# Transformer block on one core: other places for the first operands of the second MLP product, the weight scales, one attention step and three squares

## The chip, the core and the metric

The kernel runs on one core of a Trainium2 chip. Its engines work side by side, each through its own queue of instructions: TensorE (PE in the profile) multiplies matrices, VectorE (DVE), ScalarE (ACT) and GpSimd (POOL) do the elementwise work, SyncE (SP) issues nearly all of the transfers. The metric is the device time of one execution in microseconds (us), the median of several runs.

## The reference

One block of a transformer over 1024 rows of width 1024, all in float32, then a last norm:

```
n = rms_norm(h, norm1_g)
qa, ka, va, qb, kb, vb = split(n @ w_in)
ya = mixer_a(qa, ka, va, sinks)      # sliding window, 8 heads on 2 kv heads
yb = mixer_b(qb, kb, vb, rel_bias)   # own chunk and 8 chunks before, 8 heads
y  = concat(rms_norm(ya, out_norm_a_g), rms_norm(yb, out_norm_b_g))
h  = h + y @ w_out
u  = square(relu(rms_norm(h, norm2_g) @ w_ff1))   # 1024 x 4096
h  = h + u @ w_ff2
return rms_norm(h, final_norm_g)
```

## The kernel before

Both MLP products are done in the manner of Strassen: seven products of half-size blocks in place of eight, numbered 1 to 7, with sums and differences of blocks as operands. Each operand is scaled by a power of two and split into a high and a low part in float16, and one product of such operands is 24 matmuls. The inner dimension of the MLP, 4096, is worked in eight groups n = 0 to 7 of 512. X names the operands from the rows of the normalised input (S, F their sums, `tp` the transposes that they come from); W and T those from the first weight; U those from u, the result of the first product; V and Z those from the second weight; C the sums of the output. `f` is the PSUM tile of the first product, `f_a` and `f_c` are those of the second.

The time falls into stages. Up to 376 us run the first projection and the two attentions, with the output projection of mixer A (`op_A`) interleaved with the last pair of heads of mixer B. Then come the projection of mixer B, the second norm, and the making of X, up to 463. From there to 729 runs the first MLP product, group after group, in the order 1, 5, 6, 3, 7, 2, 4 within a group (the groups 0 and 1 are interleaved). From 729 runs the second.

The two halves of group 7's products are followed by those of group 0 and 1 of the second product, whose operands must be there at 729: u for n = 0 and 1 (`u0_1` is u of group 0 as product 1 reads it), loaded back from the memory `ud`, where each group stored it, and blocks of the second weight (`w2_0_00` is block (0, 0) of group 0). `fetch2` issues a u load, `load2w` a weight load, and `prepare2(i)` the scaling and splitting of the i-th product's U and V: U's high part is made by ScalarE after it has scaled u (line 1416, 1418; under one line, 153, while in written order), U's low part by GpSimd (line 1420) or, for product 5, by VectorE, and V's low part by VectorE (line 1422). `m2` (in short m) are loads of the second weight from which only its largest entry is found, by squaring on ScalarE; they are issued by `look2`, one per product, and `scale2` makes the scale of them.

What sets the order: TensorE's instructions stand in the written order. Through the first product SyncE, and from its ninth product on ScalarE, are wrapped in `InOrder`, so that they issue as written too; VectorE, GpSimd and the rest go by a scheduler's estimate, with manual dependencies where the code adds one. A wait on such an engine holds all that stands behind it. In `product1`, VectorE adds product 6, 7 or 2 to the kept sum (line 1481) and squares what is above zero (line 1482).

Some further names: `ts_vB` is the second half of the values of the last pair of mixer B, times the row norm (line 443); `y` the output of mixer A, split for the projection (line 929 on VectorE, 926 on ScalarE); `o` its result (line 1077); `nm_B` the row maximum of the scores `S_B`; `G_B` the transposed probabilities and `VvB` the transposed values, both made by DMA. The function `scaled1` scales the weights of group n; `split` makes high and low part.

Of the kernel before, what the change touches and what calls it, by code (L numbers as in the profile page):

```python
# [35 lines left out]
AHEAD1 = 2  # L36
AT_ONCE = 3
AHEAD2 = 2
LOAD2 = 5
LOOK_AHEAD = 2  # L40
START_FILL = 3
A_FILL = 7
B_FILL = [13, 13, 9.5, 9.5] * 2 + [11.25] * 8
# [3 lines left out]
SPLIT_FIRST = {(1, 1, 2): 0, (1, 1, 5): 1}  # L47
SPLIT_AT = {(0, 0): (2, 0), (0, 2): (3, 0), (2, 1): (0, 1), (2, 3): (1, 1), (2, 5): (2, 1), (2, 7): (3, 1)}
POOL_NORM = ((1, 0), (1, 1))
FIRST_BLOCK = ((0, 0), (1, 0), (0, 1), (1, 1), (2, 0), (2, 1), (3, 0), (3, 1))  # L50
EARLY = 7
P_UP = 14
PLACES = ((4, 0, 6, 12), (0, 10, 20, 30))
# [6 lines left out]
def kernel(  # L60
# [37 lines left out]
    def f(ap):  # L98
        return ap.bitcast(F32)
# [324 lines left out]
                    for rep in range(2):  # L424
                        nc.sync.dma_start(f(dst[2 * hl + s][rep * HD : (rep + 1) * HD]), src)

    freed = []

    def behind_values(ins):

        if freed:
            dep = mybir.DependencyInfo(mybir.DependencyClass.NoSync, mybir.DependencyReason.DATA)
            tc.add_manual_dep(ins.ins, freed[0], dep, reason="program order")

    def values_b(acc, name, dst, t):

        if t == 0:
            if name == "vB3":
                halves[name] = page([P, 2, HALF], f"ts_{name}", F32)
            else:  # L440
                halves[name] = main.tile([P, 2, HALF], F32, tag="tst", bufs=TST, name=f"ts_{name}")
        st = halves[name]
        ins = nc.vector.tensor_tensor(st[:, t], acc, R1[:, t * HALF : (t + 1) * HALF], ALU.mult)
        if (name, t) == ("vB3", 1):
            freed.append(ins.ins.name)
        if t == 0:
            return
        st = st.rearrange("p a b -> p (a b)")
        top, e, up, down = (small.tile([P, 1], F32, tag=f"v{i}", bufs=2, name=f"{i}_{name}") for i in ("top", "e", "up", "down"))
        nc.vector.tensor_reduce(top, st, mybir.AxisListType.X, ALU.max, apply_absolute_value=True)  # L450
        nc.vector.tensor_scalar(top, top, 2.0**-90, None, ALU.max)
        nc.vector.tensor_scalar(e.bitcast(I32), top.bitcast(I32), 0xFF << 23, None, ALU.bitwise_and)
        nc.vector.tensor_scalar(
            up.bitcast(I32), e.bitcast(I32), -1.0, float((254 + V_UP) << 23), ALU.mult, ALU.add
        )
        nc.vector.tensor_scalar(
            down.bitcast(I32), e.bitcast(I32), 1.0, -float((V_UP + P_UP) << 23), ALU.mult, ALU.add
        )
        m = 4 + int(name[2:])
        gain = small.tile([P, 1], F32, tag="vgain", bufs=2, name=f"gain_{name}")  # L460
        nc.vector.tensor_tensor(gain, down, ogc[:, m : m + 1], ALU.mult)
        pieces = page([P, 2, SEQ], f"h{name}", F16)
        nc.scalar.activation(pieces[:, 0], st, AF.Copy, scale=up)
        nc.vector.scalar_tensor_tensor(pieces[:, 1], st, up, pieces[:, 0], ALU.mult, ALU.subtract)
        V = page([P, TB, 2, 2, HD], f"V{name}", F16)
        for s in range(2):
            for hl in range(2):
                nc.sync.dma_start_transpose(V[:, :, s, hl], pieces[s * HD : (s + 1) * HD, hl])
        dst.extend([V, down, gain])
# [349 lines left out]
    class UnitB:  # L819
# [96 lines left out]
        def end(self):  # L916
            p = self.pair
            y = p.rows(self.t)[self.s * HD : (self.s + 1) * HD]
            nc.scalar.activation(y, self.av[HD:], AF.Copy)
            behind_values(nc.vector.tensor_tensor(y, self.av[:HD], y, ALU.add))  # L920
            if self.s:
                p.finish(self.t)

# [38 lines left out]

    def split_ya(m, t):
        y = ys_a[m][t]
        behind_values(split_y(y, f(y[:, 1]), ogc[:, m : m + 1]))

    def out_weight(m):

# [81 lines left out]
    def out_proj_a():  # L1050
        ys, ws = ys_a, []
        for m in range(4):
            ys.append([load_ya(m, 0)])
        for m in range(4):
            ws.append(out_weight(m))
        yield
        for tb in range(TB):
            if tb == 1:
                for m in range(4):
                    ys[m].append(load_ya(m, 1))  # L1060
            h = hres[tb] = page([P, D], f"h{tb}", F32)
            nc.sync.dma_start(h, x[tb * P : (tb + 1) * P, :])
            ps = {}
            for n in range(8):
                q, dh = FIRST_BLOCK[n] if tb == 0 else (n % 4, n // 4)
                if (tb, n) in SPLIT_AT:
                    split_ya(*SPLIT_AT[tb, n])
                c = slice(dh * HALF, (dh + 1) * HALF)
                if q == 0:
                    ps[dh] = aps.tile([P, HALF], F32, tag="w", bufs=2, name=f"op_A_{tb}_{dh}")  # L1070
                out_proj_step(ps[dh], ys, ws, q, tb, c)
                last = (tb, n) == (TB - 1, 7)
                if last:
                    yield
                if q == 3:
                    o = main.tile([P, HALF], F32, tag="tst", bufs=TST, name=f"o{tb}_{dh}")
                    nc.scalar.activation(o, ps[dh], AF.Copy, scale=rA[:, tb : tb + 1])  # L1077
# [293 lines left out]
        nc.vector.tensor_tensor(down1[n], down1[n], xdown, ALU.mult)  # L1371
        to_scale1[n] = up1, [(0, 0), (0, 1), (1, 1), (1, 0)]

    to_scale1, last_w = {}, []

    def scaled1(n, *blocks):
        up1, left = to_scale1[n]
        for b in blocks:
            if b in left:
                left.remove(b)  # L1380
                w = w1s[(n, *b)]
                ins = act1[0].activation(w, w, AF.Copy, scale=up1)
                if last_w:
                    dep = mybir.DependencyInfo(mybir.DependencyClass.NoSync, mybir.DependencyReason.DATA)
                    tc.add_manual_dep(ins.ins, last_w[0], dep, reason="program order")

    def page1(shape, name, dt=F32):
        return page(shape, name, dt)
# [23 lines left out]
    def split(full, name, engine, alloc, up=None):  # L1412
        w = alloc(name)
        w = [w[:, hl] for hl in range(2)]
        if up is not None and engine is pool:
            act1[0].activation(full, full, AF.Copy, scale=up)  # L1416
            up = None
        last_w[:] = [act1[0].activation(w[0], full, AF.Copy, scale=1.0 if up is None else up).ins.name]  # L1418
        if up is None:
            engine.tensor_tensor(w[1], full, w[0], ALU.subtract)  # L1420
        else:
            engine.scalar_tensor_tensor(w[1], full, up, w[0], ALU.mult, ALU.subtract)  # L1422
        return w
# [19 lines left out]
    def product1(n, p):  # L1443
# [32 lines left out]
        if p == 4:  # L1476
            act1[0].activation(v, ps, AF.Relu)
            act1[0].activation(v, v, AF.Square)
            dve.tensor_reduce(top, ps, mybir.AxisListType.X, ALU.max)
        else:  # L1480
            dve.tensor_tensor_reduce(v, ps, v, 1.0, 0.0, ALU.add, ALU.max, top)  # L1481
            dve.scalar_tensor_tensor(v, v, 0.0, v, ALU.max, ALU.mult)
# [173 lines left out]
    for at, (n, p) in enumerate(order1):  # L1656
        if at == 8:
            act1[0] = InOrder(nc.scalar)
        if p == (1 if n > 1 else 5) and n:
            load1(n + 1)  # L1660
        ahead1 = at + (AHEAD1 + 1 if at < AT_ONCE else AHEAD1)

        behind = (n, p) == (0, 2)
        if ahead1 < len(order1) and not behind:
            prepare1(*order1[ahead1], ahead1)
        product1(n, p)
        for work in chores.get((n, p), ()):
            combined(*work)
            if behind and work[0] == 5:
                prepare1(*order1[ahead1], ahead1)  # L1670
        if 0 < n < NQ - 1:
            if p == 3:
                see1(n + 1)
            if p == 7:
                scale1(n + 1)
        if p == 3 and n and n % GQ == 0:
            scale_of_u(n // GQ - 1)
        if at > 6:
            look2(at, n < 2 or p not in (1, 5))
        if n == NQ - 1:  # L1680
            if p in (1, 5):
                for tile2 in blocks2(0)[(p == 5) * 4 :][:4]:
                    load2w(*tile2)
            if p == 6:
                for i in range(LOAD2 - 1):
                    fetch2(i)
            for i in {7: (0,), 2: (1, 2, 3)}.get(p, ()):
                prepare2(i)
    assert not to_see and not on_way and not to_scale
    act1[0] = nc.scalar  # L1690
    acc = {}
# [3 lines left out]
            acc[i, j, n] = page([P, 2, HALF], f"C{i}{j}{n}", F32)  # L1695
            queue[0].dma_start(acc[i, j, n], hB[2 * i + n][:, :, j * HALF : (j + 1) * HALF])

    for i in range(LOAD2 - 1, LOAD2):
        fetch2(i)
    load_acc(0, 0)  # L1700
    while stores:
        stores.pop(0)()
# [245 lines left out]
```

## Time and profile before

| | us |
|---|---|
| runs | 1044.37, 1043.99, 1040.94 |
| median of them | 1043.99 |
| profiled execution | 1042.79 |
| its span | 1041.0 |
| TensorE busy in the span | 1001.6 (96%) |
| VectorE busy | 810.6 (78%) |
| ScalarE busy | 645.0 (62%) |
| GpSimd busy | 446.8 (43%) |
| mean granted clock of TensorE | 0.989 |

A row of a timeline below reads: start and length in us, engine and line, operation, output <- inputs with their sizes, how many instructions are run together in the row, and in brackets the idle time before it and what ended that. SPq is SyncE's queue, whose rows are the issuing of transfers and not the transfers. A row of a group of issues ends with the size and the median time from issue to landing.

### The profile page before, as it was taken

The page shows a single profiled execution, that of the slowest core. Times are in us where ns is not written, and L with a number is a line of the kernel's source. Part 1 is how long each engine was busy: PE and PEld are TensorE (multiplying, and loading weights), DVE is VectorE, ACT ScalarE, POOL GpSimd, SP SyncE. Part 2 cuts the span into 40 slices and gives each one's busy share as a digit, 9 for nine tenths or more (in the row PEclk, how much of TensorE's full clock was granted, in tenths as well). Part 3 has the DMA queues.
Part 4 walks back from the last instruction along what each step waited for, and adds up shares of the span by engine and source line. Part 5 has one row for each costly group of instructions (what it writes and reads, how often), then busy time and mean ns, then how long its engine had stood idle before and what let it go on. Part 6 is the DMA issues. An engine that isn't in the chain of part 4 may idle for free.

```text
span 1041.0 us, 14050 instructions
## 1 busy us (share of the span) xinstructions
PE 1001.6 (96%) x4818; PEld 591.3 (57%) x4818; DVE 810.6 (78%) x1291; ACT 645.0 (62%) x1054; POOL 446.8 (43%) x341
## 2 busy tenths in 40 slices
PE   9999999999988999989999999999889999999997
PEld 7888887777655778534444444444334444444443
DVE  6576887867686748996999987984987877686976
ACT  8676766767585836663646654754487655657446
POOL 0466665243352562106435444543164343344333
PEclk9999999999998999999999999999899999999999
DMA  9944527999999985105767757748499544443004
GB/s 357 267 121 126 141 73 184 196 217 222 216 260 213 213 268 182 61 21 182 263 223 261 237 187 278 262 168 322 176 314 402 186 158 152 172 142 122 1 1 162
DMA packets 150567, 200.63 MB, mean 193 GB/s; under 512 B 78688, under 2 KB 96224, under 8 KB 150496
## 3 DMA queue, kind: packets, MB, share of 16 engines
q1 hardware_dynamic: 150352, 199.47, 63.0%
q8 instruction: 38, 0.62, 0.3%
q14 instruction: 33, 0.27, 0.1%
q10 hardware_dynamic: 144, 0.26, 0.1%
HBM read 120.01 MB, written 42.99 MB: 157 GB/s over the span
## 4 chain that ended last, share of the span: by engine, by line
PE 50%; DVE 7%; DMA 3%; ACT 3%; issue 2%; DVEq 0%; SPq 0%; ACTq 0%
PE f L173 24%; PE f_a L173 12%; PE f_c L173 6%; PE f_b L173 4%; PE op_B L173 2%; DMA u<-ud 2%; DVE V L1422 1%; DMA G_B<-H_B 1%; DMA w<-in_w_ff_dram 1%; DVE C L1741 1%; DVE Z L1392 1%; ACT V L1418 1%; DVE W L1422 0%; DVE h L1255 0%; ACT fo L1755 0%
## 5 line engine op out<-in xcount | busy, mean ns | idle before, releaser
L173 PE MATMUL f<-X,W 128*128 128x512 f16 x1344 | 294.3, 381 | 3.1 <-DVE X L1298 3.1
L173 PEld LDWEIGHTS <-U 128*128 128x128 f16 x1356 | 133.5, 99 | 171.8 <-issue 14.9
L173 PEld LDWEIGHTS <-W 128*128 128x128 f16 x1344 | 132.0, 98 | 160.3 <-issue 5.9
L1420 POOL TENSOR_TENSOR U<-u,U 128x1024 f16<-128x1024 f32 x48 | 117.7, 2462 | 176.7 <-ACT U L1418 152.8
L173 PE MATMUL f_a<-V,U 128*128 128x512 f16 x756 | 168.1, 383 | 4.8 <-DVE topf L1481 3.7
L1420 POOL TENSOR_TENSOR W<-T,W 128x1024 f16<-128x1024 f32 x29 | 73.6, 2541 | 87.1 <-ACT W L153 45.4
L1416 ACT ACTIVATE u<-u,uupn 128x1024 f32<-128x1024 f32 x46 | 52.0, 1143 | 65.8 <-DMA u<-ud 65.7
L173 PE MATMUL f_c<-V,U 128*128 128x512 f16 x384 | 86.0, 384 | 5.0 <-DVE C L1741 3.8
L1420 POOL TENSOR_TENSOR W<-w,W 128x1024 f16<-128x1024 f32 x21 | 49.5, 2359 | 87.6 <-ACT W L153 67.0
L1422 DVE SCALAR_TENSOR_TENSOR V<-Z,up,V 128x1024 f16<-128x1024 f32 x32 | 52.6, 1646 | 26.6 <-ACT V L1418 22.0
L635 ACT ACTIVATE P_B<-P_B,nm_B 128x640 f32<-128x640 f32 (+2 forms) x64 | 44.2, 690 | 30.8 <-DVE nm_B L632 16.4
L1418 ACT ACTIVATE U<-u 128x1024 f16<-128x1024 f32 x46 | 48.2, 1047 | 23.5 <-DVE Z L1392 11.3
L173 PE MATMUL op_A<-w_o,y 128*128 128x512 f32 x192 | 57.7, 427 | 4.9 <-ACT o L1077 3.8
L880 DVE SCALAR_TENSOR_TENSOR H_B<-P_B,rc_B,H_B 128x640 f16<-128x640 f32 (+2 forms) x64 | 51.8, 836 | 12.8 <-ACT H_B L875 12.5
L1422 DVE SCALAR_TENSOR_TENSOR V<-w,up,V 128x1024 f16<-128x1024 f32 x24 | 43.3, 1804 | 20.5 <-ACT V L1418 11.9
L153 ACT ACTIVATE w<-w,up 128x1024 f32<-128x1024 f32 x24 | 26.7, 1136 | 46.7 <-DVE up L1167 46.7
L173 PE MATMUL ip_qB<-nT,w_qB 128*128 128x512 f32 x192 | 53.8, 406 | 1.1 <-DVE t_kB L409 1.0
L173 PE MATMUL ip_kB<-nT,w_kB 128*128 128x512 f32 x192 | 53.7, 404 | 0.0
L173 PE MATMUL ip_vB<-nT,w_vB 128*128 128x512 f32 x192 | 51.2, 400 | 0.0
L173 PE MATMUL ip_qA<-nT,w_qA 128*128 128x512 f32 x192 | 50.2, 395 | 0.3 <-DVE VA L179 0.3
L173 PE MATMUL S_B<-KkB,QqB 128*128 128x320 f32 (+2 forms) x192 | 41.9, 328 | 7.3 <-DVE nm_B L634 4.7
L173 PE MATMUL op_B<-w_o,y 128*128 128x512 f32 x192 | 46.8, 396 | 0.2 <-ACT o L1077 0.2
(293 smaller groups left out, 1992.2 us busy)
## 6 DMA issues: line engine op xcount, KB each, us to landing
w<-in_w_ff_dram SPq DMA_DIRECT2D x64, 512.0 KB, 7.4
u<-ud SPq DMA_DIRECT2D x56, 512.0 KB, 6.0
ud<-k SPq DMA_DIRECT2D x48, 512.0 KB, 4.5
m<-in_w_ff_dram SPq DMA_DIRECT2D x32, 512.0 KB, 5.6
KkB<-t_kB SPq DMA_DIRECT2D x32, 256.0 KB, 5.3
xr<-in_x_dram SPq DMA_DIRECT2D x8, 512.0 KB, 8.6
st_o<-in_w_out_dram SPq DMA_DIRECT2D x8, 512.0 KB, 4.9
h<-in_x_dram SPq DMA_DIRECT2D x8, 512.0 KB, 4.8
```

What stands on the lines that cost most here:

```text
L153: ins = getattr(self.engine, op)(*args, **kw)
L173: pe(nc.tensor.matmul(*args, **kw))
L635: nc.scalar.activation(pr, pr, AF.Exp, bias=nm, scale=-1.0, accum_out=sm)
L880: nc.vector.scalar_tensor_tensor(lo, q, rc, hi, ALU.mult, ALU.subtract)
L1392: engine.tensor_tensor(t, a, b, op)
L1416: act1[0].activation(full, full, AF.Copy, scale=up)
L1418: last_w[:] = [act1[0].activation(w[0], full, AF.Copy, scale=1.0 if up is None else up).ins.name]
L1420: engine.tensor_tensor(w[1], full, w[0], ALU.subtract)
L1422: engine.scalar_tensor_tensor(w[1], full, up, w[0], ALU.mult, ALU.subtract)
L1741: nc.vector.scalar_tensor_tensor(flat(c), flat(ps), down2[g], flat(c), ALU.mult, ALU.add)
```

## The change

Four parts:

1. In group 7 of the first product, the first operands of the second are loaded in another order: u and the weight blocks interleaved, two of six u loads behind products 1 and 5 already, and all six ahead of group 7's stores (`FIRST_LOADS`; `LOAD2` is 6 instead of 5). The four first calls of `prepare2` follow products 6, 3, 7 and 2, not 7, 2, 2 and 2 (`FIRST_PIECES`).
2. `look2` loads m at six of seven products of every group, all but product 1, where it had been all seven in the groups 0 and 1 and five in the others.
3. Two orders are dropped that had been fixed by hand: `behind_values`, which held some y and Y work of VectorE behind `ts_vB`, and `FIRST_BLOCK`, the order of eight pieces of the output projection's first rows; and `last_w`, which held the scaling of a weight on ScalarE behind the last split.
4. The square in group 0 after products 3, 7 and 2 is a Relu and a Square on ScalarE instead of one operation on VectorE. In all, VectorE has three instructions fewer and ScalarE six more.

```diff
-LOAD2 = 5
+LOAD2 = 6
+FIRST_LOADS = {
+    1: ((0, ((0, 0, 0), (0, 0, 1))), (2, ())),
+    5: ((1, ((1, 0, 0), (1, 0, 1))), (3, ())),
+    6: ((None, ((0, 1, 1), (1, 1, 1))), (4, ())),
+    3: ((None, ((0, 1, 0), (1, 1, 0))), (5, ())),
+}
+FIRST_PIECES = {6: 0, 3: 1, 7: 2, 2: 3}
...
-FIRST_BLOCK = ((0, 0), (1, 0), (0, 1), (1, 1), (2, 0), (2, 1), (3, 0), (3, 1))
...
-            behind_values(nc.vector.tensor_tensor(y, self.av[:HD], y, ALU.add))
+            nc.vector.tensor_tensor(y, self.av[:HD], y, ALU.add)
...
-        behind_values(split_y(y, f(y[:, 1]), ogc[:, m : m + 1]))
+        split_y(y, f(y[:, 1]), ogc[:, m : m + 1])
...
-                q, dh = FIRST_BLOCK[n] if tb == 0 else (n % 4, n // 4)
+                q, dh = (n // 2, n % 2) if tb == 0 else (n % 4, n // 4)
...
-                ins = act1[0].activation(w, w, AF.Copy, scale=up1)
-                if last_w:
...
+                act1[0].activation(w, w, AF.Copy, scale=up1)
...
-            dve.scalar_tensor_tensor(v, v, 0.0, v, ALU.max, ALU.mult)
+            if n:
+                dve.scalar_tensor_tensor(v, v, 0.0, v, ALU.max, ALU.mult)
+            else:
+                act1[0].activation(v, v, AF.Relu)
+                act1[0].activation(v, v, AF.Square)
...
-            look2(at, n < 2 or p not in (1, 5))
+            look2(at, p != 1)
         if n == NQ - 1:
-            if p in (1, 5):
-                for tile2 in blocks2(0)[(p == 5) * 4 :][:4]:
+            for i, blocks in FIRST_LOADS.get(p, ()):
+                if i is not None:
+                    fetch2(i)
+                for tile2 in blocks:
                     load2w(*tile2)
-            if p == 6:
-                for i in range(LOAD2 - 1):
-                    fetch2(i)
-            for i in {7: (0,), 2: (1, 2, 3)}.get(p, ()):
-                prepare2(i)
+            if p in FIRST_PIECES:
+                prepare2(FIRST_PIECES[p])
...
-    for i in range(LOAD2 - 1, LOAD2):
-        fetch2(i)
```

**SyncE at the boundary.** The rows of SyncE's queue behind the last store of group 6 (`ud_3_152`), first before. The numbers behind the names count buffers; 108, 115, 112, 119 and 113, 120 are u of groups 0 and 1 for products 1, 5 and 6:

```order
L153 DMA ud_3_152<-k_6_6705 128x1024
L153 DMA w_0_00_6929<-in_w_ff_dram 128x2x512
L153 DMA w_0_01_6931<-in_w_ff_dram 128x2x512
L153 DMA w_0_11_6933<-in_w_ff_dram 128x2x512
L153 DMA w_0_10_6935<-in_w_ff_dram 128x2x512
L153 DMA w_1_00_6968<-in_w_ff_dram 128x2x512
L153 DMA w_1_01_6970<-in_w_ff_dram 128x2x512
L153 DMA w_1_11_6972<-in_w_ff_dram 128x2x512
L153 DMA w_1_10_6974<-in_w_ff_dram 128x2x512
L153 DMA u_1_7010<-ud_1_108 128x1024
L153 DMA u_1_7012<-ud_1_115 128x1024
L153 DMA u_5_7014<-ud_5_112 128x1024
```

After:

```order
L159 DMA ud_3_152<-k_6_6722 128x1024
L159 DMA u_1_6950<-ud_1_108 128x1024
L159 DMA w_0_00_6952<-in_w_ff_dram 128x2x512
L159 DMA w_0_01_6954<-in_w_ff_dram 128x2x512
L159 DMA u_5_6956<-ud_5_112 128x1024
L159 DMA u_1_6988<-ud_1_115 128x1024
L159 DMA w_1_00_6990<-in_w_ff_dram 128x2x512
L159 DMA w_1_01_6992<-in_w_ff_dram 128x2x512
L159 DMA u_5_6994<-ud_5_119 128x1024
L159 DMA w_0_11_7027<-in_w_ff_dram 128x2x512
L159 DMA w_1_11_7029<-in_w_ff_dram 128x2x512
L159 DMA u_6_7031<-ud_6_113 128x1024
```

The first u load was the ninth of these loads and is the first; the second u of product 1 was the tenth and is the fifth.

**ScalarE at the same place.** Before, from the last work of group 7's product 6; W_2 and W_4 are high parts for group 7's products 2 and 4:

```order
L153 ACTIVATE k_6_7005<-f_7_1_6897 128x1024
L153 ACTIVATE m_7_10_6889,tops_w_3_6629<-m_7_10_6889 128x1024
L153 ACTIVATE W_2_7018<-w_7_10_6588 128x1024
L153 ACTIVATE W_4_7050<-T_4_7048 128x1024
L153 ACTIVATE u_1_7010<-u_1_7010,uupn_5565 128x1024
L153 ACTIVATE U_1_7094<-u_1_7010 128x1024
L153 ACTIVATE V_1_7098<-w_0_00_6929,up_0_5758 128x1024
L153 ACTIVATE u_1_7012<-u_1_7012,uupn_5567 128x1024
L153 ACTIVATE U_1_7129<-u_1_7012 128x1024
L153 ACTIVATE V_1_7133<-w_1_00_6968,up_0_5758 128x1024
L153 ACTIVATE U_5_7138<-u_5_7014,uupn_5565 128x1024
```

After:

```order
L159 ACTIVATE k_6_7025<-f_7_1_6919 128x1024
L159 ACTIVATE u_1_6950<-u_1_6950,uupn_5570 128x1024
L159 ACTIVATE U_1_7033<-u_1_6950 128x1024
L159 ACTIVATE V_1_7037<-w_0_00_6952,up_0_5716 128x1024
L159 ACTIVATE W_2_7040<-w_7_10_6618 128x1024
L159 ACTIVATE u_1_6988<-u_1_6988,uupn_5572 128x1024
L159 ACTIVATE U_1_7076<-u_1_6988 128x1024
L159 ACTIVATE V_1_7080<-w_1_00_6990,up_0_5716 128x1024
L159 ACTIVATE W_4_7085<-T_4_7083 128x1024
L159 ACTIVATE U_5_7117<-u_5_6956,uupn_5570 128x1024
L159 ACTIVATE V_5_7120<-Z_5_7115,up_0_5716 128x1024
```

The high parts W_2 and W_4 stood ahead of the first u; each now stands behind the scaling, U and V of one half.

**ScalarE where X is made.** Before, from the scaling of group 1's first weights:

```order
L1382 ACTIVATE w_1_00_4527<-w_1_00_4527,up_1_4804 128x1024
L1382 ACTIVATE w_1_01_4529<-w_1_01_4529,up_1_4804 128x1024
L1418 ACTIVATE W_1_4811<-w_1_00_4527 128x1024
L1297 ACTIVATE X_4814<-S_0_4732 128x2x256
L1297 ACTIVATE X_4815<-S_1_4762 128x2x256
L1418 ACTIVATE W_5_4822<-T_5_4820,up_0_4587 128x1024
```

After:

```order
L1377 ACTIVATE w_1_00_4527<-w_1_00_4527,up_1_4804 128x1024
L1377 ACTIVATE w_1_01_4529<-w_1_01_4529,up_1_4804 128x1024
L1377 ACTIVATE w_1_11_4597<-w_1_11_4597,up_1_4804 128x1024
L1377 ACTIVATE w_1_10_4595<-w_1_10_4595,up_1_4804 128x1024
L1410 ACTIVATE W_1_4811<-w_1_00_4527 128x1024
L1292 ACTIVATE X_4814<-S_0_4732 128x2x256
L1292 ACTIVATE X_4815<-S_1_4762 128x2x256
L1410 ACTIVATE W_5_4822<-T_5_4820,up_0_4587 128x1024
```

The scalings of w_1_11 and w_1_10, which stood 29 and 33 rows further down, now stand ahead of W_1 and X.

**VectorE in the last attention pair.** Before:

```order
L632 ISA P_B_1_3_3538,nm_B_1_3453<-S_B_1_3_3537,b_B_587 128x640
L632 ISA nm_B_1_3453 128x1
L443 TENSOR_TENSOR ts_vB_3399<-ip_vB_1_3548,R_180 128x512
L929 SCALAR_TENSOR_TENSOR y_2_3405<-y_2_3405,ogc 128x512
L920 TENSOR_TENSOR Y_0_3472<-av_B_0_3494,Y_0_3472 64x512
L929 SCALAR_TENSOR_TENSOR y_3_3407<-y_3_3407,ogc 128x512
L450 TENSOR_REDUCE top_vB_3580<-ts_vB_3399 128x1
L634 ISA P_B_0_0_3612,nm_B_0_3607<-S_B_0_0_3611,b_B_586 128x128
```

After:

```order
L925 SCALAR_TENSOR_TENSOR y_2_3405<-y_2_3405,ogc 128x512
L876 SCALAR_TENSOR_TENSOR H_B_1_1_3490<-P_B_1_0_3458,rc_B_1_3455,H_B_1_1_3490 128x640
L876 SCALAR_TENSOR_TENSOR H_B_1_1_3490<-P_B_1_1_3482,rc_B_1_3455,H_B_1_1_3490 128x640
L628 ISA P_B_1_3_3538,nm_B_1_3453<-S_B_1_3_3537,b_B_587 128x640
L628 ISA nm_B_1_3453 128x1
L925 SCALAR_TENSOR_TENSOR y_3_3407<-y_3_3407,ogc 128x512
L916 TENSOR_TENSOR Y_0_3472<-av_B_0_3494,Y_0_3472 64x512
L441 TENSOR_TENSOR ts_vB_3399<-ip_vB_1_3548,R_180 128x512
L630 ISA P_B_0_0_3612,nm_B_0_3607<-S_B_0_0_3611,b_B_586 128x128
```

`ts_vB` moved behind y_2, y_3 and the addition to Y_0, and the pair's next scores (P_B_0_0) stand right behind it, ahead of the reduction of ts_vB.

More of the change, by code (lines that the diff above doesn't have):

```diff
@@ L425, in keys_b @@
                         nc.sync.dma_start(f(dst[2 * hl + s][rep * HD : (rep + 1) * HD]), src)
[L427 to L433, printed above, removed]
     def values_b(acc, name, dst, t):
@@ L442, in values_b @@
         st = halves[name]
-        ins = nc.vector.tensor_tensor(st[:, t], acc, R1[:, t * HALF : (t + 1) * HALF], ALU.mult)
-        if (name, t) == ("vB3", 1):
-            freed.append(ins.ins.name)
+        nc.vector.tensor_tensor(st[:, t], acc, R1[:, t * HALF : (t + 1) * HALF], ALU.mult)
         if t == 0:
@@ L1372, in scale1 @@
         to_scale1[n] = up1, [(0, 0), (0, 1), (1, 1), (1, 0)]
-    to_scale1, last_w = {}, []
+    to_scale1 = {}
     def scaled1(n, *blocks):
@@ L1381, in scaled1 @@
                 w = w1s[(n, *b)]
-                ins = act1[0].activation(w, w, AF.Copy, scale=up1)
-                if last_w:
-                    dep = mybir.DependencyInfo(mybir.DependencyClass.NoSync, mybir.DependencyReason.DATA)
-                    tc.add_manual_dep(ins.ins, last_w[0], dep, reason="program order")
+                act1[0].activation(w, w, AF.Copy, scale=up1)
     def page1(shape, name, dt=F32):
@@ L1417, in split @@
             up = None
-        last_w[:] = [act1[0].activation(w[0], full, AF.Copy, scale=1.0 if up is None else up).ins.name]
+        act1[0].activation(w[0], full, AF.Copy, scale=1.0 if up is None else up)
         if up is None:
```

## The prediction

> **What bounds the kernel now.** I read the page first, for the engines' shares.
>
> ```profile
> PE 1001.6 (96%) x4818; PEld 591.3 (57%) x4818; DVE 810.6 (78%) x1291; ACT 645.0 (62%) x1054; POOL 446.8 (43%) x341
> ```
>
> TensorE is the bound: an edit pays only where it removes idle time of PE, or a slow clock behind such idle time. So the second view is PE's timeline, which shows each run of matmuls, the idle time ahead of it and what ended that. Around the boundary of the two MLP products:
>
> ```profile
> 719.12 10.52 PE L173 MATMUL f<-X,W 128*128 128x512 f16 x48
> 729.48 2.75 PE L173 MATMUL f_a<-V,U 128*128 128x512 f16 x12
> 735.98 10.47 PE L173 MATMUL f_a<-V,U 128*128 128x512 f16 x36 [3.74 <-DVE topf L1481]
> 746.29 10.52 PE L173 MATMUL f_c<-V,U 128*128 128x512 f16 x48
> 767.89 2.75 PE L173 MATMUL f_c<-V,U 128*128 128x512 f16 x12 [0.47 <-DVE C L1741]
> 773.95 9.62 PE L173 MATMUL f_c<-V,U 128*128 128x512 f16 x36 [3.31 <-DVE C L1741]
> 783.40 8.80 PE L173 MATMUL f_a<-V,U 128*128 128x512 f16 x40
> ```
>
> A pair of products (48 matmuls) takes 729.48 − 719.12 = 10.36 us at full speed. Four pairs from 729.48 would end at 770.92, but the fifth starts at 783.40: 12.5 us are lost, 7.5 in the three waits shown and 5.0 at a slow clock. The third view, a table by stage (columns: length, PE, PEld, DVE, ACT and POOL busy, then the granted clock, DMA share and GB/s), shows the clock and the stage between:
>
> ```profile
> 463.00:719.00 256.00, 256.00 (x1193) 117.11 (x1192) 220.90 (x265) 145.79 (x177) 120.78 (x49) 1.00 0.66 228
> 310.00:320.00 10.00, 10.00 (x42) 6.75 (x42) 5.73 (x17) 7.63 (x18) 0.18 (x2) 0.83 0.97 191
> 330.00:340.00 10.00, 9.78 (x44) 7.26 (x45) 8.54 (x13) 7.52 (x15) 5.24 (x4) 0.83 1.00 227
> 440.00:450.00 10.00, 7.69 (x38) 3.52 (x36) 10.00 (x15) 5.46 (x7) 0.00 (x0) 1.00 0.00 2
> 450.00:460.00 10.00, 7.31 (x28) 2.87 (x25) 10.00 (x16) 6.09 (x10) 0.00 (x0) 0.83 0.13 52
> 730.00:740.00 10.00, 6.26 (x21) 2.37 (x20) 10.00 (x12) 6.30 (x7) 1.25 (x1) 0.72 0.00 1
> ```
>
> From 463 to 719 PE never stops; no edit there can gain. A granted 0.83 over 10 us costs 1.7 us, and it follows waits of over 2 us, as below.
>
> **The boundary, first loads ahead of the stores.** The 3.74 us are for a PSUM bank that the addition for product (7,2) frees on DVE. That stands behind V's low half, which waits for ScalarE, which waits for u:
>
> ```profile
> 706.71 5.26 SPq L153 DMA_DIRECT2D w<-in_w_ff_dram  x8
> 712.51 4.71 SPq L153 DMA_DIRECT2D u<-ud  x4
> w<-in_w_ff_dram SPq DMA_DIRECT2D x1, 512.0 KB, 5.7
> u<-ud SPq DMA_DIRECT2D x4, 512.0 KB, 10.7
> 723.63 1.15 ACT L153 ACTIVATE u<-u,uupn 128x1024 f32<-128x1024 f32 x1 [10.83 <-DMA u<-ud]
> 727.01 2.15 DVE L1422 SCALAR_TENSOR_TENSOR V<-w,up,V 128x1024 f16<-128x1024 f32 x1 [5.17 <-issue]
> 729.15 3.18 DVE L1392 TENSOR_TENSOR Z<-w,w 128x1024 f32<-128x1024 f32 x1
> 734.70 1.21 DVE L1481 CUSTOM_DVE_ANT_0 k<-f,k 128x1024 f32<-128x1024 f32 x1
> 725.95 2.13 POOL L1420 TENSOR_TENSOR U<-u,U 128x1024 f16<-128x1024 f32 x1 [9.81 <-ACT U L153]
> ```
>
> The rows with KB are DMA issues, with the median us to landing. The first 512 KB block issued at 706.71 lands at 712.4; the twelfth (the last u, issued about 717) at about 727.5, so one lands every 1.35 us. In the new order u0_1 is first and lands at 712.4 instead of 723.6, and u1_1 is fifth: 717.8. ScalarE then makes u (1.15), U (1.06) and V (1.13) for half 0 by 715.7, and the W of (7,2) by 716.8; for half 1 by 721.1, and the W of (7,4) by 722.1. DVE's part for (7,2) then runs at about 731 and not 734.70, one bank time after 729.48, so the 3.74 us shrink to 0–0.5. The next u's (product 6) are loaded ahead of the stores and no longer behind them, so the 0.47 and 3.31 us, which are C's additions late behind late U and V, go as well: by my walk C is done at 756–759, needed at 761.
>
> What it newly risks: the W of (7,2) and (7,4) stand on ScalarE behind the waits for u0_1 and u1_1, and their low halves on POOL behind U's (2.13 each). The low half of (7,2)'s W is ready at 716.8 + 2.13 = 718.9 or later, needed at 719.6; that of (7,4)'s at 724.2 or later, needed at 724.8. DVE and POOL delay one another here: the V row at 727.01 took 2.15 instead of 1.27 with a POOL row under way until 728.08. Three to four such DVE operations now fall between POOL's, 1.2 us each. I take 2.0 us of new waits on PE (bounds 0, the two free slots; 4, all four operations in series). Boundary: 12.5 − 0.5 − 2.0 = **10 us gained** (5.5 to 12).
>
> On SP the stores of group 7 stood behind twelve loads and now stand behind fourteen; only later products read them, and C's loads keep their place behind the first of them. LOAD2 = 6 brings one load of 512 KB forward, 1.35 us of the transfers: nothing.
>
> **m at six products.** The m blocks' loads, squares and scales come earlier; the amount of work is the same. Cover: the row 463:719, PE 256.00 of 256.00 with ScalarE busy 145.79. Cost 0. If a W came just in time, one more square and its read (1.05 + 0.19 by rows of their kind) would cost 1.24 us per group, 7.4 over six groups: the upper bound.
>
> **X stage: two scalings earlier, squares off DVE.**
>
> ```profile
> 442.76 0.63 PE L176 MATMUL tp<-ident,n 128*128 128x128 f32 x4 [1.89 <-DVE S L1325]
> 453.35 8.97 PE L173 MATMUL f<-X,W 128*128 128x512 f16 x33 [2.69 <-DVE X L1298]
> 431.34 2.19 ACT L1382 ACTIVATE w<-w,up 128x1024 f32<-128x1024 f32 x2 [0.60 <-DVE up L1167]
> 449.68 1.21 DVE L1482 SCALAR_TENSOR_TENSOR k<-k 128x1024 f32<-128x1024 f32 x1
> 451.42 1.28 DVE L1334 TENSOR_TENSOR S<-F,S 128x512 f32<-128x512 f32 x2
> ```
>
> DVE is busy 10.00 of 10.00 here, so PE's wait at 453.35 falls with whatever leaves DVE ahead of that X: the square (1.21) and two sums that now stand behind it (1.28), 2.5 us less. ScalarE gets 2.19 us of scaling ahead of W and X at 433, and a Relu and a Square (about 1.05 each) ahead of one X: I give back 0.5 on each path. PE then waits about 2.4 instead of 1.89 and 0.7 instead of 2.69, and with no long wait the clock of 450:460 stays at 1.00: 1.7. Sum: 2.0 − 0.5 + 1.7 = **3 us gained** (0.5, if ScalarE's work eats it, to 4). The two other squares (1.2 off DVE each, 2.1 on ScalarE) lie after 463, where nothing waits: 0.
>
> [...]
>
> **Attention: values' order put back.**
>
> ```profile
> 301.82 0.96 PE L173 MATMUL op_A<-w_o,y 128*128 128x512 f32 x3 [1.07 <-DVE ts_vB L443]
> 309.77 0.73 PE L173 MATMUL S_B<-KkB,QqB 128*128 128x512 f32 x2 [2.27 <-DVE nm_B L634]
> 330.22 0.96 PE L173 MATMUL op_A<-w_o,y 128*128 128x512 f32 x3 [3.81 <-ACT o L1077]
> 301.07 0.69 DVE L443 TENSOR_TENSOR ts_vB<-ip_vB,R 128x512 f32<-128x512 f32 x1
> 301.68 0.97 DVE L929 SCALAR_TENSOR_TENSOR y<-y,ogc 128x512 fp32r<-128x512 f32 x1
> 302.68 0.69 DVE L920 TENSOR_TENSOR Y<-av_B,Y 64x512 f32<-64x512 f32 x1
> 327.83 0.72 ACT L926 ACTIVATE y<-y,ogc 128x512 fp32r<-128x512 f32 x1 [3.78 <-DMA y<-ya]
> 329.50 0.67 ACT L1077 ACTIVATE o<-op_A,rgA 128x512 f32<-128x512 f32 x1
> 315.44 5.17 SPq L468 DMA_TRANSPOSE VvB<-hvB  x4
> ```
>
> The values' part (ts_vB) goes behind one y, then another, and Y: 301.07 becomes about 303, so the 1.07 us become about 3.7 and the slow clock comes at 300 instead of 310. The waits for nm_B behind it (2.27 and a smaller one of 1.0) shrink to about 0.5, since PE arrives 2.6 us later for the same DVE work. On SP the four VvB transposes (5.17) now stand ahead of a G_B transpose: 0–1.5 us. Up to 326 that is about even (+0.6). Then the 3.81 us: ScalarE's o stood behind a y that waited 3.78 for a DMA; now it stands ahead, so the wait and the 0.83 of 330:340 go: 3.8 + 1.7 − 0.6 = 4.9. As this stage has short slack on five queues, I take **3 us gained** (0 to 5).
>
> **Sum.** 10 + 3 + 3 = 16. The profiled execution took 1042.79 (span 1041.0 and 1.8 around it), so 1026.8; the median of the three runs shown is 1.2 above it, so **1028 us**.
>
> **Rivals.**
> 1. The boundary keeps half. If u0_1 lands 10.7 us after issue as the u rows above, and not 5.7, it comes at 717.4; the low W of (7,2) is ready at 724.5, needed at 719.6: a wait of 5 and 1.7 of clock. The boundary then gains 3.3, the sum is 9.3: 1034.7. For it: reading what was stored may be slower than a weight. Against: those u's had eight blocks ahead of them.
> 2. Attention does not gain: the wait for ts_vB comes with its slow clock (2.6 + 1.7), nm_B's waits stay, and G_B adds 1.5, while the 3.81 us turn into a wait for the y behind it. Instead of −3 it is +2: 1033.
> 3. Gains given back: 1 and 2 together, with no gain at X, is about −1.3: 1042.7, no change.
> 4. Slower: the W's behind u on ScalarE. If u0_1 is later by L than my 712.4, PE loses L and about 3.4 us of clock (both W's). That turns 16 us of gain into a loss at L = 13, with u0_1 at 725, 18 us after its issue. The nearest row is 10.7; it needs SP to be held up ahead of that load as well. At L = 18 it is 1049.
>
> **Chances.** As forecast 0.60 (1022 to 1033), rival 1 0.18, rival 2 0.10, rival 3 0.07, rival 4 0.05. The low end takes 12, 4 and 5 (21 less: 1023) and 1 for what the walk misses; the high end reaches rivals 1 and 2 with 2 us for m. About 0.3% (3 us) is what a measurement of this kernel can tell from no change. Faster by more: 0.60 + 0.18 + 0.10 = 0.88; within: 0.07; slower: 0.05.
>
> **What would show it.** Right: u0_1's scaling on ScalarE starts near 713, no wait over 1.5 us between 719 and 785 on PE, its clock there 1.00, the fifth pair 9–12 us sooner after the first; PE resumes at X after a wait below 1.5; no wait for o at 330. Wrong: PE waits for W inside (7,2) or (7,4); waits of 2 us or more for ts_vB and for nm_B; PE idle between 463 and 719.

## The result and the profile after

The changed kernel takes 1031.32 us (median of 4 runs, 1029.93 to 1032.67), the kernel before 1043.09 in the same comparison: a ratio of 0.990, with a 95% interval from 0.9879 to 0.9922. The medians differ by 11.8 us; the ratio stands for 10.4. 1028 was forecast, with 1022 to 1033 for the case as forecast and up to about 1037 with rivals 1 and 2. A profile is of one execution: the one of the changed kernel took 1032.67, the longest of its four, with a span of 1030.9, so the two spans differ by 10.1 us, and the parts below are made up against that. The page's row for the engines' shares:

```profile
PE 998.8 (97%) x4818; PEld 592.0 (57%) x4818; DVE 799.7 (78%) x1288; ACT 650.6 (63%) x1060; POOL 447.2 (43%) x341
```

TensorE is busy 2.8 us less with the same matmuls: that is mostly slow clock that went (mean granted clock 0.992, before 0.989). The rest is idle time. PE's timeline at the boundary, as read before:

```profile
699.78 22.83 PE L179 MATMUL f<-X,W 128*128 128x512 f16 x105
726.43 7.03 PE L179 MATMUL f<-X,W 128*128 128x512 f16 x24 [3.83 <-DVE topf L1473]
733.30 10.52 PE L179 MATMUL f_a<-V,U 128*128 128x512 f16 x48
764.38 10.52 PE L179 MATMUL f_c<-V,U 128*128 128x512 f16 x48
774.74 10.52 PE L179 MATMUL f_a<-V,U 128*128 128x512 f16 x48
```

Inside the second product all is as forecast: from 733.30 each pair follows the last after 10.36 us, without a wait, and at full clock. But one product earlier, ahead of (7,4), stands a wait that the forecast does not have: 3.83 us, for the addition (line 1473) that frees a PSUM bank, and 24 matmuls in 7.03 us and not 5.2 behind it. Product 4 adds to the PSUM tile that product 7 has written, so it cannot start before the addition for product 7 has read that tile. (Such additions are made on VectorE for the products 3, 7 and 2; product 6 is copied by ScalarE.) The other waits of PE of over 0.8 us between 300 and 600:

```profile
304.48 2.93 PE L179 MATMUL op_A<-w_o,y 128*128 128x512 f32 x6 [4.03 <-DVE ts_vB L441]
345.39 0.85 PE L179 MATMUL S_B<-KkB,QqB 128*128 128x320 f32 x4 [1.64 <-DVE nm_B L628]
369.22 0.48 PE L179 MATMUL av_B<-G_B,VvB 128*128 128x384 f16 x2 [1.22 <-DMA G_B<-H_B]
439.57 0.66 PE L182 MATMUL tp<-ident,n 128*128 128x128 f32 x4 [1.97 <-ACT F L1312]
507.28 20.46 PE L179 MATMUL f<-X,W 128*128 128x512 f16 x94 [0.87 <-POOL W L1412]
592.02 0.32 PE L182 MATMUL all_w<-ident,top_w 128*128 128x128 f32 x1 [1.68 <-DVE top_w L1189]
```

The wait for o at 330 and the one for X at 453 are gone; ts_vB waits longer; and at 507 and 592, in the stage where PE never stopped before, stand two new ones.

Why the bank was late is read from the three engines' timelines at that place, VectorE first, then GpSimd and ScalarE, and last the u load's row of DMA issues:

```profile
712.67 2.21 DVE L1414 SCALAR_TENSOR_TENSOR V<-w,up,V 128x1024 f16<-128x1024 f32 x1 [7.16 <-ACT V L159]
719.02 3.15 DVE L1384 TENSOR_TENSOR Z<-w,w 128x1024 f32<-128x1024 f32 x1
722.10 3.14 DVE L1414 SCALAR_TENSOR_TENSOR V<-w,up,V 128x1024 f16<-128x1024 f32 x1
725.16 1.21 DVE L1473 CUSTOM_DVE_ANT_0 k<-f,k 128x1024 f32<-128x1024 f32 x1
...
718.54 2.55 POOL L1412 TENSOR_TENSOR U<-u,U 128x1024 f16<-128x1024 f32 x1 [1.67 <-ACT U L159]
721.05 3.10 POOL L1412 TENSOR_TENSOR W<-T,W 128x1024 f16<-128x1024 f32 x1
...
709.30 1.15 ACT L159 ACTIVATE u<-u,uupn 128x1024 f32<-128x1024 f32 x1 [1.18 <-DMA u<-ud]
...
u<-ud SPq DMA_DIRECT2D x1, 512.0 KB, 4.5
```

The u load itself came sooner than forecast: it was issued at 704.82 and not 706.71, and landed 4.5 us later and not 5.7. The addition for product 7 of group 7 needs product 7, which ended at about 717.4, and a kept sum that was long there. It stood on VectorE behind Z and V of the second piece, which nobody needs before the second product, and each of these took over 3 us, beside an operation of GpSimd, where such operations take 1.2 elsewhere.

By stage, from the waits above and those of before (a half clock for 3.4 us, called a dip below, costs 1.7). The wait near 980 is this one of the kernel before:

```profile
981.64 10.52 PE L173 MATMUL f_c<-V,U 128*128 128x512 f16 x48 [1.24 <-ACT V L1418]
```

| stage | lost before | lost after | gained | forecast |
|---|---|---|---|---|
| attention, 299 to 400 | 8.5 + 3.4 of clock | 7.1 + 3.4 | 1.4 | 3 |
| X | 5.0 + 1.7 | 2.0 + 1.7 | 3.0 | 3 |
| first product, 463 to (7,2) | 0 | 2.55 | -2.55 | 0 |
| boundary | 12.5 | 3.8 + 1.7 | 7.0 | 10 |
| second product, near 980 | 1.2 | 0 | 1.2 | 0 |

The sum is 10.05, the spans differ by 10.1. Each row compares one execution with one other; how far that carries for attention is said further down.

### The profile page after: what moved, and what is told of

Same layout as the page of the kernel before. It is cut to its first block, busy times and chain, and to the rows that moved or that the text cites. A ratio compares the mean times of both kernels' runs of the same rounds, so it can differ in the third digit from the quotient of the medians.

```text
span 1030.9 us, 14057 instructions
## 1 busy us (share of the span) xinstructions
PE 998.8 (97%) x4818; PEld 592.0 (57%) x4818; DVE 799.7 (78%) x1288; ACT 650.6 (63%) x1060; POOL 447.2 (43%) x341
## 4 chain that ended last, share of the span: by engine, by line
PE 46%; DVE 7%; issue 4%; DMA 3%; ACT 2%; POOL 2%; SPq 0%; DVEq 0%; POOLq 0%; ACTq 0%
PE f L179 17%; PE f_a L179 14%; PE f_c L179 7%; PE f_b L179 4%; PE op_B L179 2%; DMA w<-in_w_ff_dram 2%; POOL W L1412 2%; DVE X L1293 1%; DMA G_B<-H_B 1%; DVE T L1384 1%; DVE W L1414 1%; DVE V L1414 1%; DVE Z L1384 1%; PE op_A L179 1%; DVE h L1250 0%
## 5 line engine op out<-in xcount | busy, mean ns | idle before, releaser
L1412 POOL TENSOR_TENSOR U<-u,U 128x1024 f16<-128x1024 f32 x48 | 119.9, 2509 | 166.8 <-ACT U L1410 152.7
L179 PE MATMUL f_a<-V,U 128*128 128x512 f16 x756 | 165.3, 379 | 1.0 <-DVE C L1734 1.0
L1410 ACT ACTIVATE V<-Z,up 128x1024 f16<-128x1024 f32 x30 | 34.1, 1138 | 20.7 <-DVE Z L1384 20.1
```

Of the source, the lines that this page charges most:

```text
L179: pe(nc.tensor.matmul(*args, **kw))
```

## The experiments

Each ratio is to the kernel before in the same comparison; the changed kernel's is 0.990, with 2.2 us to either side, so differences of 2 or 3 us from it are not clear of the intervals. All edits are to the changed kernel unless the text says otherwise.

**Part 1 undone** (the loads and pieces of before):

```diff
-            for i, blocks in FIRST_LOADS.get(p, ()):
...
+            if p in (1, 5):
+                for tile2 in blocks2(0)[(p == 5) * 4 :][:4]:
+                    load2w(*tile2)
+            if p == 6:
+                for i in range(LOAD2 - 1):
+                    fetch2(i)
```

> The changed kernel with its first part undone: the loads, the pieces and LOAD2 = 5 of before at the boundary; m at six products, attention and X as changed. Theory: the first part took 12.5 us of loss away and put a wait of 3.8 us and 1.7 us of slow clock in, so 7 us net, and another 1.2 us late in the second product: undone, about 1039 us, with the waits of 3.7 and 3.3 us back and no wait of 3.8 us ahead of product (7,4). Rival: the 3.8 us wait comes from m or from the phase of the stage and stays: 1043 us or more.

Measured 0.9959 (0.9945 to 0.9973), 1039.7 us. PE's timeline:

```profile
732.77 10.78 PE L179 MATMUL f_a<-V,U 128*128 128x512 f16 x36 [3.23 <-DVE topf L1473]
770.60 7.93 PE L179 MATMUL f_c<-V,U 128*128 128x512 f16 x36 [3.30 <-DVE C L1737]
979.61 10.70 PE L179 MATMUL f_c<-V,U 128*128 128x512 f16 x41 [3.08 <-DVE C L1737]
```

The two old waits are back and the new one ahead of (7,4) is gone, as the theory has it: the wait of 3.83 us belongs to part 1. With 0.006 of 1043 us, part 1 is worth about 6 us, less than the 7.0 and 1.2 of the table, and the wait at 979 is part of it. At 979 stands a wait of 3.08 us where the changed kernel has none.

**Part 2 alone**, on the kernel before:

```diff
-            look2(at, n < 2 or p not in (1, 5))
+            look2(at, p != 1)
```

> The kernel before with only the second part of the change: m at six of seven products. Theory: it costs the two new waits in the first product, 0.9 and 1.7 us, so 1045.5 us against 1043. Rival: those waits come from the three earlier parts, which shift PE against VectorE in that stage; then m alone has no wait between 463 and 719 and takes 1043 us, no change.

Measured 1.0012 (0.9997 to 1.0026): the time does not tell the theories apart, nor a loss from none; the timeline does in part.

```profile
596.35 0.32 PE L183 MATMUL all_w<-ident,top_w 128*128 128x128 f32 x1 [1.68 <-DVE top_w L1200]
```

The 1.68 us come with part 2 and nothing else: the transpose `all_w`, which PE runs for the scale that m gives, stands at 596.35 and waits, where in the kernel before the same transpose starts at 604.40 without a wait. The wait of 0.87 for W does not appear here, nor in the next two kernels, so it is not m's alone; with part 1 undone it is there, at 0.89. What else it needs stays open.

**Part 3's attention orders put in again** (`behind_values` and `FIRST_BLOCK`).

> The changed kernel with the two hand-made orders of the attention stage put in again (VectorE's y work behind the values, and the order of the first eight pieces). Theory: the two together gained 2 us, so 1033.3 us, with the waits of 1.1, 2.3 and 3.8 us back, and with 3.4 us of slow clock as before. Rival: the forecast 3 to 5 us: 1035 us. Second rival: the later stages absorb it and the time stays at 1031.

Measured 0.9921 (0.9892 to 0.9949), 2.2 us more than the changed kernel's ratio. That is the theory's size, but the intervals overlap and hold the two rivals too. The waits of 1.62 for ts_vB, 0.96 and 2.96 for nm_B and 3.25 for o are back; a wait of 2.89 at 979.06 is there as well, so not all of the 2.2 need be attention's.

**The X stage of before** (`last_w`, and the squares on VectorE).

> The changed kernel with the third scaling order and the squares on VectorE put in again (X stage as before). Theory: worth 3.0 us: 1034.3 us, with the wait for X of about 2.7 us back and the slow clock moved behind it. Rival: ScalarE's extra work eats it, and it is worth 0.5 us or less: 1031.5.

Measured 0.9954 (0.9939 to 0.9969): 5.6 us by the ratios, more than expected.

```profile
451.50 8.75 PE L179 MATMUL f<-X,W 128*128 128x512 f16 x32 [2.69 <-DVE X L1293]
978.25 12.04 PE L179 MATMUL f_c<-V,U 128*128 128x512 f16 x48 [3.09 <-DVE C L1733]
```

The wait for X is back with its clock, the 3.0 us of the theory. The rest is the second row: the wait near 979 again, with 1.7 us of clock. By the ratios the three parts undone come to 6.2, 2.2 and 5.6 us, 14.0 in all, and the whole change to 10.4 with m's loss of 1.2 to add: 2.4 too much, which the intervals do not clear of noise. The traces show what would count twice: three of these kernels wait about 3 us near 979, where the changed kernel doesn't wait. The orders of VectorE, ScalarE and GpSimd in the second product are the same in x3_old_attention as in the changed kernel, so it isn't an order; what sets that wait was not found.

**Is the wait the bank?** VectorE's work for the first pieces held behind the bank's addition, and the second piece prepared after product 7, so that (7,4)'s W stands ahead of u1_1 on ScalarE:

```diff
-FIRST_PIECES = {6: 0, 3: 1, 7: 2, 2: 3}
+FIRST_PIECES = {6: (0,), 7: (1,), 2: (2, 3)}
...
+            added = dve.tensor_tensor_reduce(v, ps, v, 1.0, 0.0, ALU.add, ALU.max, top)
+            if (n, p) == (NQ - 1, 7):
+                bank_free.append(added.ins.name)
...
+        if engine is dve and bank_free and len(bank_free) == 1:
+            dep = mybir.DependencyInfo(mybir.DependencyClass.NoSync, mybir.DependencyReason.DATA)
+            tc.add_manual_dep(ins.ins, bank_free[0], dep, reason="program order")
```

> The changed kernel with V, U and Z work of VectorE for the first second-product pieces held behind the addition of group 7's product 7, which frees the bank for product (7,4); the second piece is prepared one product later, so that W of (7,4) stands ahead of u1_1 on ScalarE. Theory (the 3.83 us wait is the bank, held by VectorE's queue): no wait of over 1 us ahead of product (7,4), clock 1.00, 5.5 us less than the changed kernel: ratio to before 0.985, 1025.5 to 1028 us on the first chip's scale. Rival: the boundary is bound by the landing of u and the sum of work on VectorE; then the wait reappears ahead of the second product (f_a or f_c, 3 us or more) and the time stays at 0.990.

Measured 0.9899 (0.9862 to 0.9936): no gain. The wait ahead of (7,4) is gone and the second product starts at 726.37, but then:

```profile
758.49 2.75 PE L179 MATMUL f_c<-V,U 128*128 128x512 f16 x12 [0.88 <-DVE C L1742]
771.98 12.17 PE L179 MATMUL f_a<-V,U 128*128 128x512 f16 x48 [2.58 <-DVE C L1742]
```

0.9, 0.2 and 2.6 us and 1.7 of clock are 5.4, where the changed kernel lost 5.5. The cause of the wait was right, what it is worth was wrong: the rival's half held, for a wait inside the second product and not ahead of it. VectorE is busy 42 of 45 us from 735 to 780 in both. This suggests that the second product of the changed kernel runs without a wait in part because the bank has made PE late for it. (The edit also holds back VectorE's work for the first pieces; r3_squares7, further down, does not, and waits for C as well.)

**GpSimd out of the way, first try.** The low half of U for the second piece issued later:

```diff
+        if name == "U1_1":
+            later.append(lambda: engine.tensor_tensor(w[1], full, w[0], ALU.subtract))
...
+        while later and p == 7:
+            later.pop()()
```

> The changed kernel with one operation of GpSimd moved: the low half of U for the second piece (half 1, product 1) is issued behind product 7's work, so GpSimd is idle while VectorE makes Z and V ahead of the bank's addition; VectorE's order is the same. Theory (VectorE's two-input operations wait while GpSimd runs one, 1.9 us each here): Z takes 1.2 instead of 3.15 us, the addition at 725.2 comes 3 us earlier, and the wait ahead of product (7,4) falls from 3.8 to about 1 us. Rival (VectorE is late for its inputs, ScalarE's V or the loads): Z's and V's ends stay, and the wait stays over 3 us.

Measured 0.9913 (0.9887 to 0.9938). GpSimd still ran that operation first (at 718.16, ahead of W's at 720.97), and the wait was 4.2 us. The edit did not do what it should, so it tells nothing of the cause.

**More work off VectorE.** The squares of group 7 on ScalarE too:

```diff
-            if n:
+            if 0 < n < NQ - 1:
                 dve.scalar_tensor_tensor(v, v, 0.0, v, ALU.max, ALU.mult)
```

> The changed kernel with the fourth part carried to group 7: its three squares are a Relu and a Square on ScalarE as well, and the scheduler then puts the addition that frees the bank for (7,4) ahead of V of the second piece. Theory (at the boundary VectorE's sum of work bounds, and moving a wait only passes it on): 3.6 us and more leave VectorE between 715 and 735, the boundary's loss falls from 5.5 to 1 to 2 us: ratio to before 0.986, against 0.990 for the changed kernel. Rival (the loads of u bound the boundary): the loss stays at 5 us or more, in other places: 0.990.

Measured 0.9943 (0.9922 to 0.9964), 4.5 us more than the changed kernel's ratio: the theory of VectorE's sum fell in this form. VectorE's work between 705 and 735 did fall, from 22.8 to 17.2 us, and the addition no longer holds the bank, but PE then waits inside the second product (2.15, 1.59 and 0.2 us for C). Then the six low halves of U on VectorE:

```diff
-            split(a, f"U{n}_{p}", dve if p == 5 else pool, high, uup[n]), split(b, f"V{n}_{p}", dve, high, up2[g])
+            split(a, f"U{n}_{p}", dve if p == 5 or 3 < at < 10 else pool, high, uup[n]), split(b, f"V{n}_{p}", dve, high, up2[g])
```

> As r3_squares7, with the low halves of U for products 6, 3 and 7 of the second product's first group (six operations) on VectorE instead of GpSimd. Theory (VectorE's two-input operations stand still while GpSimd runs one, so GpSimd's work costs VectorE nearly as much as its own): VectorE's rows between 735 and 775 all take 1.2 to 1.3 us instead of up to 3.2, its busy time there rises by less than 3 us, and PE loses no more than in r3_squares7 plus 2 us. Rival (no such coupling; the long rows have another cause): 6 x 1.27 = 7.6 us more on VectorE, and PE loses 5 to 8 us more.

Measured 0.988 (0.9853 to 0.9907), against 0.9943 in the same comparison, with intervals that don't touch. First r3_squares7: two of PE's waits, the stage from 735 to 780 (length, PE, PEld, DVE, ACT, POOL busy, clock, DMA share, GB/s), and groups of VectorE's rows in it (count, busy us, mean ns, idle before):

```profile
724.91 4.92 PE L179 MATMUL f<-X,W 128*128 128x512 f16 x22 [2.67 <-POOL W L1412]
763.07 12.21 PE L179 MATMUL f_c<-V,U 128*128 128x512 f16 x48 [2.15 <-DVE C L1734]
...
735.00:780.00 45.00, 41.03 (x182) 17.92 (x180) 42.31 (x31) 28.89 (x29) 24.14 (x9) 0.96 0.96 306
...
L1414 DVE SCALAR_TENSOR_TENSOR V<-w,up,V 128x1024 f16<-128x1024 f32 x4 | 10.7, 2724 | 2.6 <-ACT V L1410 2.6
L1384 DVE TENSOR_TENSOR Z<-w,w 128x1024 f32<-128x1024 f32 x2 | 4.4, 2181 | 0.0
L1734 DVE SCALAR_TENSOR_TENSOR C<-f_c,down,C 128x1024 f32<-128x1024 f32 x2 | 2.5, 1272 | 0.0
```

And r7_u_low_vector, the same views:

```profile
725.33 4.92 PE L179 MATMUL f<-X,W 128*128 128x512 f16 x22 [2.65 <-POOL W L1412]
972.08 12.21 PE L179 MATMUL f_c<-V,U 128*128 128x512 f16 x48 [3.01 <-DVE C L1734]
...
735.00:780.00 45.00, 45.00 (x210) 20.40 (x209) 41.53 (x43) 25.71 (x25) 7.43 (x4) 1.00 0.99 325
...
L1414 DVE SCALAR_TENSOR_TENSOR V<-w,up,V 128x1024 f16<-128x1024 f32 x4 | 6.0, 1509 | 2.8 <-ACT V L1410 2.8
L1384 DVE TENSOR_TENSOR Z<-w,w 128x1024 f32<-128x1024 f32 x2 | 2.4, 1210 | 0.0
L1734 DVE SCALAR_TENSOR_TENSOR C<-f_c,down,C 128x1024 f32<-128x1024 f32 x4 | 5.1, 1274 | 0.0
```

VectorE does 43 operations instead of 31 in the stretch and is busy 0.8 us less; V falls from 2724 ns to 1509, Z from 2181 to 1210; C, one of whose inputs is in PSUM, takes 1.27 us both times. PE's waits between 735 and 780 are all gone; one of 3.01 us near 972 takes the place of one of 2.12 in r3_squares7. So the 16.7 us of GpSimd's work that left the stretch had cost VectorE about as much as doing it itself. (The edit also takes six scalings of u from ScalarE, 3.2 us of its busy time here; how much of PE's gain is theirs was not separated.) In both kernels the 2.65 us ahead of (7,4) that are left are for W on GpSimd: the forecast's own risk, hidden in the changed kernel behind the bank.

**Attention, taken apart.** The values' order put in again, the new piece order kept:

> The changed kernel with VectorE's y work held behind the values again, but the new order of the eight pieces kept. Theory (the dropped hand order costs, the new piece order gains): the wait for ts_vB falls from 4.0 to about 1 us and the slow clock at 303 to half or none, the wait for o at 330 stays away: 3 us less than the changed kernel, ratio 0.987. Rival (the wait only moves on to nm_B or G_B): the waits for nm_B and G_B grow by what ts_vB loses, ratio 0.990.

Measured 0.9928 (0.9893 to 0.9963), no gain. PE's and ScalarE's rows:

```profile
329.65 1.65 PE L179 MATMUL op_A<-w_o,y 128*128 128x512 f32 x3 [5.33 <-ACT o L1082]
327.69 1.33 ACT L932 ACTIVATE y<-y,ogc 128x512 fp32r<-128x512 f32 x2 [5.50 <-DMA y<-ya]
```

ts_vB's wait falls to 1.77, but the wait for o is back: with the new order of the pieces, the values' order decides whether the scheduler puts o ahead of y on ScalarE. The order of the pieces alone does not bring it about. Then o was put ahead by hand as well:

```diff
+        if o_last and not wait:
+            dep = mybir.DependencyInfo(mybir.DependencyClass.NoSync, mybir.DependencyReason.DATA)
+            tc.add_manual_dep(ins.ins, o_last[0], dep, reason="program order")
```

> The changed kernel with VectorE's y work held behind the values again, and on ScalarE the y's of the second half held behind the o that stands before them in the program. Theory (part 3 gained by putting o ahead of y on ScalarE and lost by putting ts_vB back on VectorE; the piece order does nothing): the wait for ts_vB is 1.8 us instead of 4.0, no wait for o over 1 us at 330, half the slow clock; 3 us less than the changed kernel: 0.987. Rival (y of the second half is then late for op_A of the third row block): a wait for y of 2 us or more between 331 and 345: 0.990.

Measured 0.9922 (0.9902 to 0.9942):

```profile
302.51 1.67 PE L179 MATMUL op_A<-w_o,y 128*128 128x512 f32 x6 [2.03 <-DVE ts_vB L449]
311.11 0.74 PE L179 MATMUL S_B<-KkB,QqB 128*128 128x512 f32 x2 [2.98 <-DVE nm_B L640]
328.60 0.96 PE L179 MATMUL op_A<-w_o,y 128*128 128x512 f32 x3 [0.84 <-ACT o L1087]
```

Both waits are about as the theory has them, and the rival's wait for y is not there; the gain went into the wait for nm_B, which the changed kernel does not have there. Not faster.

**Two combinations.** Bank first with values first, and r3_squares7 with r4_o_first:

> The two edits together: the bank's addition first, and the values first. If both theories hold the gains add: 8 us less than the changed kernel, ratio 0.982. If one of the rivals holds, the sum is that of the other alone.

> r3_squares7 and r4_o_first in one. If both theories hold, their gains add: 7 us less than the changed kernel, ratio 0.983, 1025 us. If only one holds, its ratio alone.

Measured 0.994 (0.9921 to 0.9959) and 0.9966 (0.9952 to 0.9981), both above the changed kernel's ratio, the second clear of the intervals: the gains do not add. No version tried beats it beyond its interval; r7_u_low_vector, at 0.988, is the nearest.

## Why the prediction was right, and where it was not

- **The boundary, mis-sized: 10 forecast, 7.0 measured.** The u's landed early, and the waits of 3.74, 0.47 and 3.31 us and their slow clock are gone, but not only by the path given. In z1_bank_first, where the second product starts at 726.37 and not 733.30, waits for C of 0.9, 0.2 and 2.6 us stand inside it, and in r3_squares7, where it starts at 729.67, such waits of 2.15, 1.59 and 0.2: "C is done at 756–759, needed at 761" did not hold where PE came on time. Two things in the step "what it newly risks" failed. It priced the W's behind u (2.0 us, bounds 0 to 4; the 2.65 us of the two kernels without the bank's wait show that this was fair), and missed the third instruction that (7,4) waits for, the addition for product 7. And it took VectorE and GpSimd to delay one another by 1.2 us in three or four operations; at 719 and 722 it was 1.9 each, and V's operations took 2.7 us between 735 and 780 until GpSimd's work was taken away. r7_u_low_vector, with both put right, loses 2.65 us here up to 780, 10 less than the kernel before. A slow clock behind a wait for (7,4) was priced in the rivals and not in the sum.
- **m at six products, wrong: 0 forecast, 1.7 measured in the trace** (2.55 with the wait for W, whose cause is open; m_alone's 1.2 by the ratio is not clear of none). "PE 256.00 of 256.00" covers what hides behind matmuls; it does not cover a transpose that PE itself runs for the scale and that part 2 put earlier in PE's queue, ahead of the VectorE work that it needs.
- **X, right in size by another path, and so in part by luck.** The wait at 453 is not shortened to 0.7 but gone; the dip of 1.7 is not gone but follows the wait at 439.57 instead. In x1_old_boundary, with the same X code, that wait brings no dip, and waits of 0.65, 0.24 and 0.35 us for S and X follow in its place.
- **Attention, right in kind, and in size by more than one pair of profiles.** ts_vB at 4.03 against 3.7, o's wait gone, G_B 1.22 in a range of 0 to 1.5. The step "about even up to 326" took one dip of 1.7: the longer wait brought two steps at half clock, 3.4 us. The table's 1.4 is of one pair. From the first matmul of `op_A` to the first transpose `tp` of the second norm, the three traces with the old orders (before, m_alone, x3_old_attention) take 97.8, 99.5 and 99.3 us, and the seven with both new orders 95.3 to 97.1, the changed kernel 95.9. The means are 2.9 us apart, against 3 forecast. The prediction named only "it now stands ahead" for o; x5_values_first shows that this hangs on the values' order.
- **Second product near 980:** 1.2 us gained that no step has. The waits there follow from something upstream that the runs did not isolate.

Of the prediction's own signs, u0_1's scaling near 713 (709.30), the fifth pair 9 to 12 us sooner after the first (12.5) and no wait for o came about. No wait over 1.5 us between 719 and 785 did not, and PE idle between 463 and 719, a sign of being wrong, did. That the sum was 16 and the two profiled executions differ by 10.1 is mostly the boundary (3.0) and m (2.55), with attention (1.6 in this pair) in the same sense and 980 (1.2) against it.

## What to carry to other kernels

When work is moved ahead of a deadline, list everything that the instruction at that deadline waits for, the release of its PSUM bank included, and look what now stands ahead of each on its engine. A wait that is removed while the engine behind it is nearly full can come back a few products later: z1_bank_first lost 5.4 us where 5.5 had been, with VectorE busy 42 of 45 us. Where VectorE and GpSimd work on the same stretch, add GpSimd's time to that of VectorE's operations with both inputs in SBUF before deciding who does what: 16.7 us of GpSimd's work gave way to six more such operations here, and VectorE was busy 0.8 us less. And read a stage from more than one execution: attention gained 2.0 us from its first to its last matmul in one pair of traces and 2.9 over ten.

## What the runs showed of the hardware

The clock. The table by stage, with its edges laid on the clock's own steps of 3.41 us (columns: length, PE busy, clock, DMA share, GB/s), for the kernel before, then the changed one, then x1_old_boundary:

```profile
440.79:444.20 3.41, 1.52 (x10) 1.00 0.00 0
444.20:447.62 3.42, 3.42 (x18) 1.00 0.01 2
451.03:454.44 3.41, 1.09 (x6) 1.00 0.38 154
454.44:457.86 3.42, 3.42 (x10) 0.50 0.00 0
...
436.76:440.17 3.41, 1.44 (x9) 1.00 0.00 0
440.17:443.59 3.42, 3.42 (x12) 0.50 0.00 0
590.40:593.80 3.40, 1.78 (x9) 1.00 1.07 370
593.80:597.20 3.40, 3.40 (x18) 1.00 1.03 419
...
434.79:438.20 3.41, 1.96 (x12) 1.00 0.00 0
438.20:441.61 3.41, 2.24 (x13) 1.00 0.00 0
```

The granted clock is 1.00 or 0.50 and nothing between, for whole steps on a fixed grid, and it follows the share of the step before in which PE was busy: 1.09 and 1.44 of 3.41 us halve the next step, 1.52 and 1.78 do not. In the traces of the kernel before and of the changed one, ten full-clock steps were followed by a half-clock one, with PE busy for 0.01 to 0.42 of them, and none in which it was busy for 0.44 or more. In the fourteen traces of this case a full-clock step with PE busy for under 0.40 of it was followed by a half-clock one every time (41 steps), one with over 0.49 never; in between both occur, so that another measure than these rows may decide there. The same wait, 1.97 us in the changed kernel and 2.0 in x1_old_boundary, costs a dip in the former, where it lies within one step (1.44 busy), and none in the latter, where it lies across two (1.96 and 2.24).

VectorE beside GpSimd. The groups above, with 24.1 us of GpSimd's work in the stretch and with 7.4, show 2.7 us against 1.5 for V and 2.2 against 1.2 for Z, both with two inputs in SBUF, and no change for C (1.27), whose other input is in PSUM. In the changed kernel Z at 719.02 and V at 722.10 took 3.15 and 3.14 us; the operations of GpSimd that were under way when they started ended at 721.09 and 724.15, and Z and V each 1.1 us after that, about the 1.2 to 1.3 that such an operation takes with GpSimd idle. The forecast had put this at 1.2 us for three or four operations; at 719 and 722 it was 1.9 each.
